# A causal convolution in a loop of 12 outputs from four half-size convolutions, with loads apart from transposes and four weight sums by ScalarE and accumulating DMA

## The chip, the core and the metric

The kernel runs on one core of a Trainium2 chip. A core has a matmul engine (TensorE, PE in the profile; its weight loads are PEld), three engines for elementwise work (VectorE is DVE, ScalarE is ACT, GpSimd is POOL), an engine that issues transfers (SyncE, SP) and 16 DMA engines. They run side by side and wait for one another through semaphores. The on-chip memory SBUF has 128 partitions. Matmul results land in PSUM, which has eight banks of 512 fp32 numbers per partition. The metric is device time in microseconds (us). "Span" is the time from the first to the last instruction of one profiled execution.

## What is computed

```python
# x [8, 4096, 512] f32, kernel [8, 512, 512] f32
def reference(x, kernel):
    out = np.zeros_like(x)
    for k in range(8):
        shifted = x delayed by k positions, zeros in front
        out += np.matmul(shifted, kernel[k])
    return out
```

This is a causal convolution over 4096 positions with 8 taps, in which each tap is a 512 x 512 matrix. Both kernels cut the 8 x 4096 positions into 128 runs of 256, one run per partition. One step of time, for all 128 runs at once, is a 128 x 512 matrix. Multiplied by one weight matrix it is called a *product* here: 4 matmuls of 128 x 128 by 128 x 512, one for each quarter of the inner 512.

## The kernel before

Eight outputs with eight taps would take 64 products. The kernel saves some of them by sums. A *node* is a convolution of 4 outputs with 4 taps, half the size, and it takes 9 products instead of 16 (names `a1 a0 u v0 v1 l00 l01 l10 l11`). Three nodes make 8 outputs: LO and HI, which work on sums of inputs with the lower and upper taps, and MID, which works on the inputs with the taps' difference. Four of the outputs are LO plus MID, the other four HI minus MID. In exchange, VectorE makes the sums of inputs and of results. All is bf16 but the results.

```python
def product(bank, comp, w, start):                 # 4 matmuls into one PSUM bank (line 197)
    for c in range(DC):
        nc.tensor.matmul(bank, lhsT=comp[:, c * P:(c + 1) * P], rhs=w[:, c, :],
                         start=start and c == 0, stop=c == DC - 1, skip_group_check=True)

def tt(o, a, b, op):                               # each VectorE sum (line 76)
    nc.vector.tensor_tensor(out=o, in0=a, in1=b, op=op)

def load_x(i, h):                                  # 4 steps of x, fp32 to bf16, into SBUF; 2 buffers
    xin[i, h] = xpool.tile([P, 4, D], bf, name="xin")
    load(xin[i, h], xr[:, K * i + 4 * h:K * i + 4 * h + 4, :])     # gpsimd DMA (line 80)

def transpose_x(i, h):                             # SBUF to SBUF, by DMA
    nc.sync.dma_start_transpose(
        out=XT[:, 4 * h:4 * h + 4, :].rearrange("p j (c m) -> p (j c) m", m=P),
        in_=xin[i, h].rearrange("p j d -> p (j d)"))

def node_seed(n, b_):                              # ScalarE: PSUM to PSUM, 512 wide
    n.p[b_] = pair((2 * n.k + b_) % 3)             # two banks; three pairs go round, a fourth is q
    ...
def node_d(n, b_):                                 # VectorE: difference in PSUM, 512 wide
    ...
def node_e(n, b_):                                 # results out of PSUM
    ...
    elif n.a == MID:
        ms[b_] = mpool.tile([P, 2, D], f32, name="ms")
        nc.scalar.copy(out=ms[b_], in_=p)
    else:
        tt(y, p, ms[b_], ADD if n.a == LO else SUB)                # 1024 wide, fp32
        store(n.i, n.a, b_, y)

# --- cut: the start, in which the first 16 outputs (6 nodes) are laid out by hand ---
for k, (i, a) in enumerate(order):                 # one turn is one node's slot
    ...
    node_l(cur, 0, LO); node_l(cur, 0, HI)         # products of this node ...
    node_a0(nxt); node_u(nxt)                      # ... mixed with those of the next
    node_l(cur, 1, LO); node_e(cur, 0)
    node_seed(nxt, 0); node_seed(nxt, 1); node_dts(nxt)
    ...                                            # prep_*: 39 rows of 512 bf16 summed per 8 outputs
    node_v(nxt, b_); node_d(nxt, b_)               # for b_ in 0, 1
    node_l(cur, 1, HI); node_a1(k + 2); node_e(cur, 1)
```

Of the kernel before, what the change touches and what calls it, by code (L numbers as in the profile page):

```python
# [8 lines left out]

LO, HI, MID = 0, 1, 2


@with_exitstack
def kernel(
# [13 lines left out]
    NIT = RUN // K  # L37
    assert K == 8 and D == 512 and S % RUN == 0 and RUN % K == 0
# [13 lines left out]
    xpool = ctx.enter_context(tc.tile_pool(name="x", bufs=2))  # L52

    ctx.enter_context(tc.manual_schedule())

    W = {}
    for a in (LO, HI, MID):
        for b_ in (LO, HI, MID):
            for c_ in (LO, HI, MID):
                W[a, b_, c_] = wpool.tile([P, DC, D], bf, name=f"w{a}{b_}{c_}")  # L60

    XT = spool.tile([P, K, D], bf, name="XT")
    D4 = spool.tile([P, K, D], bf, name="D4")
    D42 = spool.tile([P, K, D], bf, name="D42")
    D421 = spool.tile([P, K, D], bf, name="D421")
    D41 = spool.tile([P, 4, D], bf, name="D41")
    D2 = spool.tile([P, 5, D], bf, name="D2")
    D21 = spool.tile([P, 4, D], bf, name="D21")
    D1 = spool.tile([P, 2, D], bf, name="D1")

    F21 = spool.tile([P, 4, D], bf, name="F21")
    F0 = spool.tile([P, D], bf, name="F0")
    A1 = spool.tile([P, 2, D], bf, name="A1")
# [4 lines left out]

    def load(out, src):
        nc.gpsimd.dma_start(out=out, in_=src)  # L80

    xin = {}

    def load_x(i, h):
        xin[i, h] = xpool.tile([P, 4, D], bf, name="xin")
        load(xin[i, h], xr[:, K * i + 4 * h:K * i + 4 * h + 4, :])

    def transpose_x(i, h):
        nc.sync.dma_start_transpose(
            out=XT[:, 4 * h:4 * h + 4, :].rearrange("p j (c m) -> p (j c) m", m=P),  # L90
            in_=xin[i, h].rearrange("p j d -> p (j d)"))


    def pairs(z):
        return z.rearrange("p (a b) d -> p a (b d)", b=2)

    def prep_m():

        tt(D1[:, 0:2], XT[:, 7::-7], XT[:, 0:2], ADD)
        tt(pairs(D2[:, 1:5]), pairs(XT)[:, 3::-3], pairs(XT)[:, 0:2], ADD)  # L100

    def prep_d27():
        tt(D2[:, 0], XT[:, 5], XT[:, 7], ADD)

    def prep_d21():
        tt(D21[:, 0:4], D2[:, 0:4], D2[:, 1:5], ADD)

    def prep_d4(h):
        a, b = (XT[:, 4:8], XT[:, 0:4]) if h == LO else (XT[:, 0:4], XT[:, 4:8])
        tt(D4[:, 4 * h:4 * h + 4], a, b, ADD)  # L110

    def prep_d41(h):
        if h == LO:
            tt(D41[:, 0:2], D4[:, 7::-7], D4[:, 0:2], ADD)
        else:
            tt(D41[:, 2:4], D4[:, 3:5], D4[:, 4:6], ADD)

    def prep_d42(h):
        if h == LO:
            tt(pairs(D42)[:, 0:2], pairs(D4)[:, 3::-3], pairs(D4)[:, 0:2], ADD)  # L120
        else:
            tt(D42[:, 4:8], D4[:, 2:6], D4[:, 4:8], ADD)

    def prep_d421(h):
        if h == LO:
            tt(D421[:, 0:4:2], D42[:, 7:0:-6], D42[:, 0:4:2], ADD)
            tt(D421[:, 1:4:2], D42[:, 0:4:2], D42[:, 1:4:2], ADD)
        else:
            tt(D421[:, 4:8], D42[:, 3:7], D42[:, 4:8], ADD)

    ppool = ctx.enter_context(tc.tile_pool(name="p", bufs=1, space=PSUM))

    def pair(k):
        return ppool.tile([P, 2, D], f32, name=f"pp{k}")

    H, HF = XT, D421.bitcast(f32).rearrange("p (t b) d -> p t (b d)", b=2)
    nc.sync.dma_start(out=HF, in_=xr[:, RUN - 4:RUN, :])
    load_x(0, 0)
    zero = spool.tile([P, D], bf, name="zero")
    nc.vector.memset(zero, 0.0)  # L145
    U1 = zero
# [5 lines left out]
    def mid(level, u, v):  # L152

        if level == 0:
            return W[MID, u, v], W[HI, u, v], W[LO, u, v]
        if level == 1:
            return W[u, MID, v], W[u, HI, v], W[u, LO, v]
        return W[u, v, MID], W[u, v, LO], W[u, v, HI]

    def mid_dve(*which):  # L160
        o, u, v = mid(*which)
        tt(o, u, v, SUB)


    def mid_neg(u, v):
        nc.scalar.mul(out=W[MID, u, v], in_=W[LO, u, v], mul=-1.0)

    def mid_acc(u, v):
        nc.gpsimd.dma_start(out=W[MID, u, v], in_=W[HI, u, v], accum_op=ADD)

    load_w(4)
    load(H[:, 1:4], xr[:, RUN - 7:RUN - 4, :])
    ident = spool.tile([P, P], bf, name="ident")
    make_identity(nc, ident)
    bank = {}

    def fill(pw):

        for h in range(2):
            nc.tensor.matmul(pw[:, h], lhsT=zero[:, 0:P], rhs=zero, start=True, stop=True)  # L180

# [7 lines left out]

    for k in range(6):  # L190
        fill(pair(k % 4))
    XF = D42


    def product(bank, comp, w, start):
        for c in range(DC):
            nc.tensor.matmul(bank, lhsT=comp[:, c * P:(c + 1) * P], rhs=w[:, c, :],  # L197
                             start=start and c == 0, stop=c == DC - 1,
                             skip_group_check=True)

    mpool = ctx.enter_context(tc.tile_pool(name="m", bufs=2))
    cpool = ctx.enter_context(tc.tile_pool(name="c", bufs=2))
    fpool = ctx.enter_context(tc.tile_pool(name="f", bufs=2))
    ypool = ctx.enter_context(tc.tile_pool(name="y", bufs=4))

    class Node:
        pass

    def streams(i, a):

        if a == MID and i == 0:
            return (F0, [D1[:, 0], D1[:, 1]], [D2[:, 1], D2[:, 3]],
                    [F21[:, j] for j in range(4)])
        if (i, a) == (1, MID):
            return (U1, [A1[:, 0], A1[:, 1]], [D21[:, 0], D21[:, 2]],
                    [F21[:, j] for j in range(4)])
        if a == MID:
            return (XT[:, 0], [D1[:, 0], D1[:, 1]], [D2[:, 1], D2[:, 3]],
                    [D21[:, j] for j in range(4)])
        o = 4 * a  # L220
        if (i, a) == (1, LO):
            return (T4[:, 0], [D41[:, 0], D41[:, 1]], [T42[:, 0], T42[:, 2]],
                    [D421[:, j] for j in range(4)])
        if (i, a) == (1, HI):
            return (D4[:, 4], [D41[:, 2], D41[:, 3]], [D42[:, 4], D42[:, 6]],
                    [D421[:, j] for j in range(4)])
        return (D4[:, o], [D41[:, 2 * a], D41[:, 2 * a + 1]], [D42[:, o], D42[:, o + 2]],
                [D421[:, o + j] for j in range(4)])

    def node_a1(k):
        n = Node()
        nodes.append(n)
        n.k, (n.i, n.a) = k, order[k]
        a = n.a  # L240
        n.s = streams(n.i, a)
        n.q = pair(3)
        product(n.q[:, 1], n.s[1][1], W[a, MID, HI], True)
        nc.scalar.copy(out=n.q[:, 0], in_=n.q[:, 1])  # L244
        n.p = {}

    def node_a0(n):
        product(n.q[:, 0], n.s[1][0], W[n.a, MID, LO], False)

    def node_u(n):  # L250
        product(n.q[:, 1], n.s[0], W[n.a, MID, MID], False)

    def node_seed(n, b_):
        n.p[b_] = pair((2 * n.k + b_) % 3)
        if b_ == LO:
            nc.scalar.copy(out=n.p[b_][:, 1], in_=n.q[:, 1])  # L256
        else:
            nc.scalar.mul(out=n.p[b_][:, 1], in_=n.q[:, 1], mul=-1.0)  # L258

    def node_dts(n):  # L260
        n.dts = cpool.tile([P, D], f32, name="dts")
        nc.scalar.copy(out=n.dts, in_=n.q[:, 0])  # L262

    def node_v(n, b_):
        product(n.p[b_][:, 1], n.s[2][b_], W[n.a, b_, MID], False)

    def node_d(n, b_):
        p = n.p[b_]
        if b_ == LO:
            tt(p[:, 0], n.dts, p[:, 1], SUB)  # L270
        else:
            nc.vector.scalar_tensor_tensor(out=p[:, 0], in0=p[:, 1], scalar=-1.0,  # L272
                                           in1=n.dts, op0=MUL, op1=SUB)

    ms = {}

    def node_l(n, b_, j):
        product(n.p[b_][:, j], n.s[3][2 * b_ + j], W[n.a, b_, j], False)

    def store(i, a, b_, y):  # L280
        t0 = K * i + 4 * a + 2 * b_
        nc.sync.dma_start(out=orr[:, t0:t0 + 2, :], in_=y)

    first = {}

    def node_y(n, b_, a):
        y = first[n.i, a, b_]
        tt(y, y, n.p[b_], ADD if a == LO else SUB)

    def node_e(n, b_):  # L290
        p = n.p[b_]
        if n.k < 4:
            pool, name = ((mpool, "ms"), (ypool, "y"), (fpool, "f"), (ypool, "y"))[n.k]
            y = pool.tile([P, 2, D], f32, name=name)
            nc.scalar.copy(out=y, in_=p)  # L295
# [40 lines left out]
    def first_run(z):  # L336

        nc.vector.memset(z[:, :, 0:D:G], 0.0)  # L338

# [308 lines left out]
```

## Time and profile before

| | |
|---|---|
| median of 3 runs | 779.75 us (779.15 to 779.77) |
| span of the profiled run | 777.3 us |
| TensorE busy | 766.8 us, 99% |
| VectorE busy | 657.5 us, 85% |
| ScalarE busy | 284.9 us, 37% |
| transposes (SyncE's queue) | 61, median 6.1 us from issue to landing |
| loads of x (GpSimd's queue) | 64 of 512 KB, median 5.9 us |

A line of groups reads: source line, engine, operation, output tile <- input tiles, partitions x elements and type, count, then busy time in us and mean ns of one, then the engine's idle time just before such instructions and what ended it. A line of the timeline reads: start in us, duration in us, engine, line, operation. A line of the chain in order of time reads: start, length, and what was running. A queue's line has its packets, its MB and its packets' time as a share of the 16 DMA engines' span.

### The profile page before, as it was taken

Reading aid. Unit: us, or ns where it says so; the run is one execution under the profiler, and the core shown is the slowest. Engines: PE = TensorE matmul, PEld = TensorE weight load, DVE = VectorE, ACT = ScalarE, POOL = GpSimd, SP = SyncE. Lnnn points to the kernel's source line nnn. Section 1 sums busy time; section 2 is a strip of 40 time slices with the busy share of each in tenths; the row PEclk is TensorE's granted clock in tenths of the full one; section 3 lists DMA queues with packets and bytes.
Section 4 is the critical chain, followed back from the end, with each engine's and each line's share of the span. In section 5 each row is a group of like instructions: output and inputs, shape, how many; then the busy total and the mean of one; then the engine's idle time right before and its main releaser. Section 6 shows DMA issues by size and latency. Waiting matters only on the chain.

```text
span 777.3 us, 9450 instructions
## 1 busy us (share of the span) xinstructions
PE 766.8 (99%) x3584; PEld 347.3 (45%) x3584; DVE 657.5 (85%) x766; ACT 284.9 (37%) x462; POOL 42.3 (5%) x80
## 2 busy tenths in 40 slices
PE   7999999999999999999999999999999999999997
PEld 3444444444444444444444444444444444444443
DVE  4999988898888898888898888898888898888895
ACT  3553343333343333343333343333343333343332
POOL 4000000000000000000000000000000000000000
PEclk9999999999999999999999999999999999999999
DMA  9986878868786877787877878877697867687843
GB/s 199 211 125 170 226 185 178 208 159 190 164 199 163 197 172 189 164 198 169 194 171 187 164 174 190 207 162 188 163 187 176 207 158 190 165 186 179 204 133 121
DMA packets 159373, 139.42 MB, mean 179 GB/s; under 512 B 130144, under 2 KB 134240, under 8 KB 159200
## 3 DMA queue, kind: packets, MB, share of 16 engines
q1 hardware_dynamic: 145456, 99.89, 46.1%
q0 software_dynamic: 13728, 38.67, 31.6%
q8 instruction: 28, 0.46, 0.2%
q10 hardware_dynamic: 144, 0.26, 0.1%
q14 instruction: 17, 0.14, 0.1%
HBM read 77.33 MB, written 67.11 MB: 186 GB/s over the span
## 4 chain that ended last, share of the span: by engine, by line
PE 96%; DMA 2%; POOL 1%; ACT 0%; issue 0%; DVE 0%; DVEq 0%; POOLq 0%
PE pp L197 96%; DMA xin<-in_x_dram 2%; POOL w L80 0%; PE pp L186 0%; ACT y L295 0%; DVE y L76 0%; DVE pp L76 0%; POOL xin L80 0%; DVEq L647 0%; ACT pp L256 0%; ACT pp L244 0%; POOL XT L80 0%; PE pp L180 0%; POOL ident masks.py:199 0%; POOL ident masks.py:197 0%
## 5 line engine op out<-in xcount | busy, mean ns | idle before, releaser
L197 PE MATMUL pp<-w,D 128*128 128x512 bf16 x3280 | 715.5, 379 | 1.3 <-DVE w L76 0.9
L197 PEld LDWEIGHTS <-D 128*128 128x128 bf16 x3280 | 320.4, 98 | 389.8 <-issue 2.8
L76 DVE TENSOR_TENSOR D<-D 128x1024 bf16<-128x1024 bf16 (+1 forms) x252 | 228.2, 945 | 1.6 <-ACT D L353 1.6
L76 DVE TENSOR_TENSOR y<-pp,ms 128x1024 f32<-128x1024 f32 (+1 forms) x121 | 146.5, 1212 | 45.5 <-PE pp L197 45.4
L76 DVE TENSOR_TENSOR D<-XT 128x2048 bf16<-128x2048 bf16 (+2 forms) x153 | 142.1, 946 | 8.5 <-DMA XT<-xin 6.7
L244 ACT COPY pp<-pp 128x512 f32<-128x512 f32 x95 | 54.1, 570 | 256.0 <-PE pp L197 256.0
L256 ACT COPY pp<-pp 128x512 f32<-128x512 f32 x95 | 54.1, 570 | 170.6 <-PE pp L197 167.6
L76 DVE TENSOR_TENSOR pp<-dts,pp 128x512 f32<-128x512 f32 x95 | 65.5, 690 | 46.2 <-ACT dts L262 44.6
L299 ACT COPY ms<-pp 128x1024 f32<-128x1024 f32 x60 | 61.0, 1016 | 33.1 <-PE pp L197 33.1
L80 POOL DMA_DIRECT2D xin<-in_x_dram x64 | 34.2, 535 | 688.3 <-DMA XT<-xin 670.6
L272 DVE SCALAR_TENSOR_TENSOR pp<-pp,dts 128x512 f32<-128x512 f32 x95 | 65.9, 693 | 3.2
L262 ACT COPY dts<-pp 128x512 f32<-128x512 f32 x95 | 57.4, 604 | 2.0 <-PE pp L197 2.0
L258 ACT ACTIVATE pp<-pp 128x512 f32<-128x512 f32 x95 | 56.0, 589 | 1.2 <-DVE y L76 1.2
L197 PE MATMUL pp<-w,XT 128*128 128x512 bf16 x120 | 30.8, 379 | 0.0
L76 DVE TENSOR_TENSOR w<-w,w 128x2048 bf16<-128x2048 bf16 x18 | 21.6, 1219 | 0.4 <-DMA w<-in_kernel_dram 0.2
L197 PEld LDWEIGHTS <-XT 128*128 128x128 bf16 x120 | 11.7, 98 | 14.2
L180 PE MATMUL pp<-zero 128*128 128x512 bf16 x24 | 8.9, 505 | 2.4 <-DVE zero L145 1.2
L197 PE MATMUL pp<-w,w 128*128 128x512 bf16 x36 | 9.0, 379 | 1.3 <-ACT pp L244 0.7
L197 PE MATMUL pp<-w,F 128*128 128x512 bf16 x36 | 8.9, 379 | 0.0
L338 DVE MEMSET D<- 128x64 bf16 x2 | 0.2, 112 | 8.2 <-ACT D L351 7.7
L80 POOL DMA_DIRECT2D w<-in_kernel_dram x8 | 6.0, 766 | 0.8 <-DMA w<-in_kernel_dram 0.8
L197 PEld LDWEIGHTS <-w 128*128 128x128 bf16 x36 | 3.5, 97 | 5.8 <-issue 2.1
(55 smaller groups left out, 70.6 us busy)
## 6 DMA issues: line engine op xcount, KB each, us to landing
out_dram<-y SPq DMA_DIRECT2D x123, 512.0 KB, 3.5
xin<-in_x_dram POOLq DMA_DIRECT2D x64, 512.0 KB, 5.9
w<-in_kernel_dram POOLq DMA_DIRECT2D x8, 512.0 KB, 15.9
D<-in_x_dram SPq DMA_DIRECT2D x1, 1024.0 KB, 4.9
out_dram<-ms SPq DMA_DIRECT2D x2, 512.0 KB, 4.2
out_dram<-f SPq DMA_DIRECT2D x2, 512.0 KB, 3.7
XT<-xin SPq DMA_TRANSPOSE x61, 6.1
w<-w POOLq DMA_DIRECT2D x1, 512.0 KB, 9.9
```

Source lines behind the costliest of these rows:

```text
L76: nc.vector.tensor_tensor(out=o, in0=a, in1=b, op=op)
L80: nc.gpsimd.dma_start(out=out, in_=src)
L180: nc.tensor.matmul(pw[:, h], lhsT=zero[:, 0:P], rhs=zero, start=True, stop=True)
L197: nc.tensor.matmul(bank, lhsT=comp[:, c * P:(c + 1) * P], rhs=w[:, c, :], start=start and c == 0, stop=c == DC - 1, skip_group_check=True)
L244: nc.scalar.copy(out=n.q[:, 0], in_=n.q[:, 1])
L256: nc.scalar.copy(out=n.p[b_][:, 1], in_=n.q[:, 1])
L258: nc.scalar.mul(out=n.p[b_][:, 1], in_=n.q[:, 1], mul=-1.0)
L262: nc.scalar.copy(out=n.dts, in_=n.q[:, 0])
L272: nc.vector.scalar_tensor_tensor(out=p[:, 0], in0=p[:, 1], scalar=-1.0, in1=n.dts, op0=MUL, op1=SUB)
L299: nc.scalar.copy(out=ms[b_], in_=p)
L338: nc.vector.memset(z[:, :, 0:D:G], 0.0)
```

## The change

The loop now makes 12 outputs per turn from four nodes of 4 outputs x 4 taps: PL (with the sum of the two halves of the taps), MI (with their difference), H1 and H0 (with one half each). The 12 outputs follow from the four results with factors of one half. The first three nodes have 9 products as before. H0 is a *leaf*: it skips the last level of sums and the `d` step and has 11 products. The first 16 outputs are still made by hand-laid nodes, and three of those six are leaves now. This is meant to lower the number of products per output.

Loads of x go to tiles of their own in device memory (`xd`), and the transposes read from there into a ring `XR` of 20 steps. A load thus no longer waits for the transpose that empties its buffer, and SBUF is free for the nine more weight matrices of PL. Four of these (the sums of two tap matrices) are a ScalarE copy followed by an adding DMA; the other sums of weights are VectorE's. The diff below is shortened, and its comments are added.

```diff
-    NIT = RUN // K
+    HEAD, STEP, R = 2 * K, 12, 20
+    NB = (RUN - HEAD) // STEP
...
-    xpool = ctx.enter_context(tc.tile_pool(name="x", bufs=2))
+    ypool = ctx.enter_context(tc.tile_pool(name="y", bufs=5))
+    dpool = ctx.enter_context(tc.tile_pool(name="xd", bufs=NB * STEP // 4, space=bass.MemoryType.DRAM))
...
+    def load_x(t):
+        if t < RUN:
+            xd[t] = dpool.tile([P, 4, D], bf, name="xd")
+            rows(xd[t], t, 4)
+    def behind(z):                     # holds GpSimd's loads back until z is written
+        nc.gpsimd.tensor_copy(out=junk, in_=z[:, 0:2])
...
+    def node_z(n):                     # VectorE, from the ring; two pieces where it wraps
+        t = n.t
+        if n.a == PL:   zsum(0, t - 3, t + 1, 7, ADD)
+        elif n.a == MI: zsum(4, t + 1, t - 3, 7, SUB)
+        elif n.a == H1: zsum(0, t - 7, t + 1, 7, SUB)
+        else:           zsum(7, t, t + 8, 4, SUB)
+    def node_A(n):
+        tt(AX[n.k % 2], n.z[:, n.o + 2:n.o + 4], n.z[:, n.o + 3:n.o + 5], ADD)
+    def node_s(n):
+        tt(SX[n.k % 2], n.z[:, n.o:n.o + 5], n.z[:, n.o + 2:n.o + 7], ADD)
+    def node_F(n, b_):                 # not in a leaf
+        ...
+            tt(F[:, 2 * b_:2 * b_ + 2], s[:, 2 * b_:2 * b_ + 2], s[:, 2 * b_ + 1:2 * b_ + 3], ADD)
...
     def node_l(n, b_, j):
+        if n.leaf:
+            for c_ in (LO, HI):
+                product(o, comps(n)[2][2 * b_ + j + c_], W[n.a, b_, c_], False)
+        else:
+            product(o, comps(n)[3][2 * b_ + j], W[n.a, b_, j], False)
...
     def node_e(n, b_):                 # 12 outputs from the four results
+        elif n.a == PL:
+            nc.scalar.mul(out=cc[b_], in_=p, mul=0.5)
+        elif n.a == MI:
+            nc.vector.scalar_tensor_tensor(out=dd[b_], in0=p, scalar=-0.5, in1=cc[b_], op0=MUL, op1=ADD)
+        elif n.a == H1:
+            tt(y, p, dd[b_], ADD)      # stored
+        else:
+            tt(dd[b_], dd[b_], p, SUB) # stored
+    def middle(n, b_):
+        nc.vector.scalar_tensor_tensor(out=cc[b_], in0=cc[b_], scalar=2.0, in1=dd[b_], op0=MUL, op1=SUB)  # stored
...
+    def seed_plus(b_, c_):
+        nc.scalar.copy(out=W[PL, b_, c_], in_=W[H1, b_, c_])
+    def add_h0(a, b_, c_):
+        nc.gpsimd.dma_start(out=W[a, b_, c_], in_=W[H0, b_, c_], accum_op=ADD)
...
+    SLOT = {   # what each node's slot issues, in order; z, A, a1 are for the node after the next
+        PL: "s l00 F1 a0 l01 u l11 e0 s0 s1 dt F0 z x A v0 d0 v1 d1 l10 a1 e1",
+        MI: "l00 s F1 a0 l01 u l11 e0 s0 s1 dt F0 z x A v0 d0 v1 d1 l10 a1 e1",
+        H1: "l00 s F1 a0 l01 u l11 e0 s0 s1 dt F0 z A r g0 v0 d0 v1 d1 l10 e1",
+        H0: "l00 s F1 b1 l01 a0 u l11 e0 s0 s1 dt F0 z x A g1 v0 d0 v1 d1 l10 a1 e1",
+    }
+    # x: two transposes in PL's slot, one in MI's; r: behind(...) and three loads, two blocks ahead; g0, g1: middle
```

The start is cut here. Its loads now come in this order: x steps 0 to 3 and 4 to 7, the last steps of the runs (for the runs that follow), taps 4 and 5, x steps 8 to 11, taps 6, 7, 3, 1, 0, 2, x steps 12 to 15. Before, it was x steps 0 to 3, tap 4, the last steps, taps 6, 5, 7, x steps 4 to 7 and 8 to 11, taps 2, 0, 3, 1.

## The prediction, made before the changed kernel ran

> **What bounds the kernel now.** I read the page from the top: busy shares first, then the chain of work that ended last, then that chain in order of time.
>
> ```profile
> PE 766.8 (99%) x3584; PEld 347.3 (45%) x3584; DVE 657.5 (85%) x766; ACT 284.9 (37%) x462; POOL 42.3 (5%) x80
> PE 96%; DMA 2%; POOL 1%; ACT 0%; issue 0%; DVE 0%; DVEq 0%; POOLq 0%
> 5.96 18.30 DMA xin<-in_x_dram
> 45.87 726.95 PE pp L197 x3364
> ```
>
> TensorE (PE) carries 96% of the chain. From 45.87 us on, the chain is one unbroken stream of 3364 matmuls in 726.95 us, 0.2161 us each. Before that the start waits for its first loads. So the time is a count of matmuls times 0.2161 us, plus a start and a tail. Line 197 has 3280+120+36+36+8+4 = 3484 matmuls in its groups (the last two are small groups of the grouping by form); 120 of them lie before 45.87 us and are worth 25.9 us. The start therefore costs 45.87 - 25.9 = 20.0 us without products, the tail 777.3 - 772.8 = 4.5 us, and 20.0 + 3484 x 0.2161 + 4.5 = 777.4, the span. The median time lies 2.4 us above the span (779.75 against 777.3).
>
> VectorE (DVE) is second at 85%. Whether it can take over is the main question, so I read its groups by form and then its starts in order of time:
>
> ```profile
> L76 DVE TENSOR_TENSOR D<-D 128x2048 bf16<-128x2048 bf16 x123 | 147.3, 1217 | 0.0
> L76 DVE TENSOR_TENSOR y<-pp,ms 128x1024 f32<-128x1024 f32 x119 | 145.2, 1221 | 45.0 <-PE pp L197 44.9
> L76 DVE TENSOR_TENSOR D<-D 128x1024 bf16<-128x1024 bf16 x127 | 81.8, 682 | 1.6 <-ACT D L353 1.6
> L76 DVE TENSOR_TENSOR pp<-dts,pp 128x512 f32<-128x512 f32 x95 | 65.5, 690 | 46.2 <-ACT dts L262 44.6 <-PE pp L197 1.4
> ```
> ```profile
> 299.50 1.22 DVE L76 TENSOR_TENSOR D<-XT 128x2048 bf16<-128x2048 bf16 x1
> 300.63 1.22 DVE L76 TENSOR_TENSOR D<-D 128x2048 bf16<-128x2048 bf16 x1
> 301.77 0.69 DVE L76 TENSOR_TENSOR pp<-dts,pp 128x512 f32<-128x512 f32 x1
> 302.37 0.69 DVE L272 SCALAR_TENSOR_TENSOR pp<-pp,dts 128x512 f32<-128x512 f32 x1
> 302.97 1.21 DVE L76 TENSOR_TENSOR D<-XT 128x2048 bf16<-128x2048 bf16 x1
> ...
> 326.29 1.21 DVE L76 TENSOR_TENSOR D<-XT 128x2048 bf16<-128x2048 bf16 x1
> ```
>
> First column start, second duration. Starts lie closer than durations: an op of 1.22 us is followed 1.14 us later, one of 0.69 us 0.60 us later. So an op costs its duration less 0.08 us in a full queue. Where an op reads what the op right before it wrote, the step is the duration plus 0.04 (the copy at 25.41 us lasts 1.23, the sum that reads it starts at 26.67). 302.97 to 326.29 is one turn of the loop: 23.32 us for 108 matmuls, 0.2159 each.
>
> **What the Trainium skill says.** "VectorE: DVE Perf Modes", section "The perf-mode tier table", gives a two-input op two elements per cycle in bf16 (1224 ns for 2048) and one with any PSUM operand or fp32; the trace agrees (1217 ns; 1221 ns for 1024 fp32). Its section "The DRAIN you can't avoid" says each op pays a flush, so count matters, and that an op which is not held starts earlier; the trace has that as the 0.08 us. "TensorE: Matmul & The Clock Gate", section "Step-by-step: what each phase is for", has 216 ns between back-to-back 512-column matmuls: here 215.9. "DMA: Bandwidth & Descriptors", section "Why small descriptors are slow (HBM only)", warns of small packets to or from device memory; the transposes move packets of about 250 B (130144 packets under 512 B for 61 transposes of 512 KB, so some 2100 each), but from SBUF here, so no run yet shows whether it bites.
>
> **The change, part by part.** *Matmuls.* A product is 4 matmuls, 0.863 us. Before, 8 outputs take 3 nodes of 9 products. After, 12 outputs take three nodes of 9 (PL, MI, H1) and one leaf of 11 (H0): 38 products. The loop has 20 x 38 x 4 = 3040 matmuls. The head of 16 outputs has the direct node (64), three leaves (3 x 44) and two nodes (2 x 36): 268. Together 3308, 176 fewer, and 176 x 0.2161 = 38.0 us are saved if PE stays full. A block of 12 then takes 152 x 0.2159 = 32.8 us.
>
> *VectorE per block*, in start-to-start cost (bf16: 0.60 for 1024; 1.14 for 2048; 0.87, 1.41 and 1.95 for 1536, 2560 and 3584 on the same slope of 0.27 us per 512; fp32: 0.60 for 512, 1.14 for 1024): six F sums 3.6; four S sums 5.6; four A sums 2.4; six d ops 3.6; the z sums 7.05 (over 20 blocks 44 of 2048, 36 of 3584, 24 of 1536, as the ring wraps); eight fp32 output ops 9.1. That is 31.4, and four A sums that read the z just written add 4 x 0.12. So 31.9 us against 32.8: VectorE goes from 85% to about 97% and just stays under PE. Per output the sums grew (65 rows per 12 against 39 per 8), the d ops fell, and a middle result needs an extra fp32 op.
>
> *Slot by slot* the two do not balance. PE has 7.8, 7.8, 5.2 and 12.1 us in the slots of PL, MI, H1 and H0; VectorE 6.5, 7.9, 8.1 and 9.3. It falls behind by about 3 us over MI and H1 and catches up in H0. Laid out by hand, with H1's slot starting at 0 and VectorE 0.8 late: it evicts H1's first pair to 3.95, ScalarE then seeds the leaf by 5.2 (leaf wanted at 6.9: fine), A of the next PL is ready at 6.65 against 6.9 when PE wants it, all later ones have over half a microsecond, and VectorE is 0.8 late again one block on. So PE-bound is possible, with a slack of 0.25 us at the tightest place. That is less than hand-over between engines can cost, so I charge 0.25 us per block: 5 us.
>
> *ScalarE per block*: 3 nodes of four 512 copies (2.3 us each), two 1024 seeds and a 512 op in the leaf (2.6), two scaled 1024 copies (2.0): 11.6 of 32.8. It does not bind.
>
> *Transposes.* Before:
>
> ```profile
> q1 hardware_dynamic: 145456, 99.89, 46.1%
> q0 software_dynamic: 13728, 38.67, 31.6%
> xin<-in_x_dram POOLq DMA_DIRECT2D x64, 512.0 KB, 5.9
> XT<-xin SPq DMA_TRANSPOSE x61, 6.1
> ```
>
> Loads and transposes share the queues' 78% and each load waits for the transpose that frees its tile. After, a load goes to its own tile in device memory, two blocks early, so that wait is gone; but it was no engine's bound. The transpose gets a new source, read a second time. Two transposes are issued after H1's z (PL's slot) and needed by the next PL's z in H1's slot, about 14 us later. Two in a row at SPq's 4.2 us issue and 6.1 us landing take some 10 to 11. They fit unless the new source is a third slower.
>
> *Start.* Four weight sums leave VectorE for a ScalarE copy (1.9 us) and a DMA (9.9 us to landing in this trace). Behind the first x, two MB-size x loads and the 3/4 MB tail rows now stand ahead of the first weight. In the trace some 7.75 MB had landed by 24.3 us, about 0.36 MB per us after 2 us of latency. The first weight (4.75 MB in) then lands near 15 us, not 11.4; the fourth (8.75 MB) near 26. By then 7 products are done (6.0 us), which leaves 20.2 us lost against 16.6 at the same point before, whose later waits made it 20.0. I take 22 us, plus 2 us for the first PL weights arriving late.
>
> *Sum.* 22 + 3308 x 0.2161 (714.9) + 4.5 + 2 + 5 = 748.4 of span, plus 2.4: **751 us**, 3.7% faster.
>
> **The rivals.** *PE stays the only bound*: no block waits and the start costs what it did: 20.0 + 714.9 + 4.5 + 2.4 = 742. For it: the slots were ordered with sums split and spread, and the hand layout closes. *VectorE becomes the bound*: it loses 3.4 us of 23.3 waiting now (45.0 + 46.2 us over the kernel), and may afford under 1 in 32.8. If waits cost 1.2 us per block beyond my charge, 24 us more: 775, level with before. Against it: those waits are those of an engine with time to spare. *The transpose from device memory is slow*: at 9 us landing, z waits some 3 us per block, and VectorE cannot make it up: +60 us, 810. Against it: the queues are 78% busy and the window is two slots. *The start eats part of it*: +5 to 8 us.
>
> **Range and chances.** 742 is a floor. Half a microsecond more per block, or a start 8 us worse, gives about 760; both together 767. Range 742 to 766. Over 2% faster means below 764.2: 0.85. Within 2% takes the VectorE rival in earnest: 0.11. Slower by 2% takes the slow transpose: 0.04.
>
> **What would show it.** Right: the chain still over 93% PE, DVE near 93 to 95% busy by page, 32.8 to 33.3 us between like instructions 12 outputs apart, landing of transposes near 6 us. Wrong: DVE or DMA with several per cent of the chain; PE idle before line 118 for DVE; z waiting for DMA; blocks over 34 us; the first product later than 18 us. Fewer than 38 us saved with full blocks would put the loss in the start.

## The result, and the profile after

| | before | after |
|---|---|---|
| median of 4 runs | 779.45 us (778.88 to 779.77) | 757.88 us (757.45 to 759.61) |
| span of the profiled run | 777.3 us | 757.9 us |
| matmuls of products | 3484 | 3308 |
| 12 outputs in the loop | 34.98 us (1.5 x 23.32) | 32.90 us |
| share of the chain held by TensorE | 96% | 88% |

The ratio is 0.9729, 95% interval 0.9716 to 0.9743: 2.7% faster. 751 us had been predicted, with a range of 742 to 766. The page of the changed kernel: busy time by engine, three rows of the forty slices, and the chain that ended last.

```profile
PE 733.4 (97%) x3352; PEld 330.7 (44%) x3420; DVE 692.0 (91%) x727; ACT 255.0 (34%) x380; POOL 62.1 (8%) x103
PE   6999689999999999999999999999999999999997
DVE  1774899999999999999999999999999999999996
PEclk9999899999999999999999999999999999999999
PE 88%; DVE 5%; DMA 4%; issue 1%; ACT 1%; POOL 0%; DVEq 0%; ACTq 0%; POOLq 0%
```

From slice 7 to the last but one both rows read 9: TensorE and VectorE are both full, as foretold. The losses stand in slices 1, 5 and 6, that is up to 20 us and from some 76 to 114 us, and in slice 5 the clock dips too. (Of 3420 matmuls issued, of which 76 are transposes and 36 fillers on zeros at the start, the trace recorded 3352. Where I count matmuls below, I take the program's count.)

Operations and transfers of the same page; the last three lines are issues with their median us to landing:

```profile
L82 DVE TENSOR_TENSOR Z<-XR 128x3584 bf16<-128x3584 bf16 (+2 forms) x104 | 147.2, 1434 | 4.1 <-DMA XR<-xd 4.1
L82 DVE TENSOR_TENSOR S<-Z 128x2560 bf16<-128x2560 bf16 x80 | 118.6, 1483 | 0.0
L247 DVE SCALAR_TENSOR_TENSOR y<-pp,y 128x1024 f32<-128x1024 f32 x40 | 48.8, 1220 | 18.2 <-PE pp L118 17.2
out_dram<-y SPq DMA_DIRECT2D x124, 512.0 KB, 7.8
xd<-in_x_dram POOLq DMA_DIRECT2D x60, 512.0 KB, 10.7
XR<-xd SPq DMA_TRANSPOSE x60, 5.1
```

Transposes from device memory land in 5.1 us, faster than the 6.1 us from SBUF before. The loads and the stores pay instead: loads went from 5.9 to 10.7 us, stores from 3.5 to 7.8 us. In the loop VectorE waits for a store once, 2.0 us at 748 us, and for no load. The sum S of 2560 elements lasts 1483 ns, a step of 1.40, where 1.41 was taken. VectorE's one regular wait is the first output op of MI's slot, 17.2 us over 20 blocks. A piece of VectorE's timeline in the steady loop (start, duration, and in brackets the idle time before the op and what ended it):

```profile
402.72 0.69 DVE L82 TENSOR_TENSOR pp<-DT,pp 128x512 f32<-128x512 f32 x1
403.32 0.69 DVE L207 SCALAR_TENSOR_TENSOR pp<-pp,DT 128x512 f32<-128x512 f32 x1
403.92 1.48 DVE L82 TENSOR_TENSOR S<-Z 128x2560 bf16<-128x2560 bf16 x1
405.32 0.68 DVE L82 TENSOR_TENSOR F<-S 128x1024 bf16<-128x1024 bf16 x1
407.02 1.23 DVE L247 SCALAR_TENSOR_TENSOR y<-pp,y 128x1024 f32<-128x1024 f32 x1 [1.02 <-PE pp L118]
...
433.02 2.02 DVE L82 TENSOR_TENSOR Z<-XR 128x3584 bf16<-128x3584 bf16 x1
435.14 0.69 DVE L82 TENSOR_TENSOR A<-Z 128x1024 bf16<-128x1024 bf16 x1
435.75 0.69 DVE L82 TENSOR_TENSOR pp<-DT,pp 128x512 f32<-128x512 f32 x1
```

The op at 402.72 comes again at 435.75. An A that reads the z just written starts 0.10 us after that z's end (435.14 against 433.02 + 2.02), where 0.04 was taken. Averaged over 15 blocks by GpSimd's small copy, which runs once in each (155.74 to 649.30), a block is 32.90 us. TensorE's 152 matmuls at 0.2159 are 32.82. So a block loses 0.08 us, and VectorE is idle about 1 us in it.

What is left is the *head*, the first 16 outputs with the start of the first block. Busy time of each engine in four stretches of 10 us; after the stretch and its length stand PE, PEld, DVE, ACT and POOL with counts, then the granted clock, the DMA engines' share and GB/s:

```profile
60.00:70.00 10.00, 9.90 (x46) 4.52 (x47) 7.14 (x9) 4.09 (x6) 0.00 (x0) 1.00 1.03 178
70.00:80.00 10.00, 7.43 (x34) 3.30 (x34) 5.87 (x7) 3.79 (x4) 0.00 (x0) 1.00 0.37 63
80.00:90.00 10.00, 7.55 (x23) 2.79 (x23) 9.42 (x11) 3.44 (x4) 1.83 (x4) 0.66 0.98 249
90.00:100.00 10.00, 6.44 (x28) 2.60 (x27) 8.49 (x9) 2.23 (x4) 2.25 (x4) 1.00 1.04 235
```

40 us at 0.2161 would hold 185 matmuls; 131 are recorded. The chain in order of time (start, length, what) shows what held it:

```profile
66.29 9.02 DMA XR<-xd
...
75.40 1.24 DVE Z L82
...
81.01 1.14 DVE w L82
...
82.17 9.31 DMA out_dram<-w
...
91.51 1.23 DVE w L82
```

A transpose takes 9 us, VectorE works 7 us, a store takes 9 us, and VectorE goes on. Until 122.8 us no matmul is in the chain, although TensorE is full again from 100 us on (busy for 9.83 us from 100 to 110 us, 9.95 from 110 to 120). The timeline has the same as a row of waits:

```profile
75.40 1.23 DVE L82 TENSOR_TENSOR Z<-XR 128x2048 bf16<-128x2048 bf16 x1 [4.10 <-DMA XR<-xd]
...
81.11 0.58 ACT L190 ACTIVATE pp<-pp 128x512 f32<-128x512 f32 x1 [3.20 <-DVE y L82]
...
81.74 3.57 PE L118 MATMUL pp<-w,S 128*128 128x512 bf16 x8 [3.89 <-ACT pp L190]
...
91.51 1.23 DVE L82 TENSOR_TENSOR w<-w,w 128x2048 bf16<-128x2048 bf16 x1 [2.09 <-DMA out_dram<-w]
...
99.69 1.02 PE L118 MATMUL pp<-w,F 128*128 128x512 bf16 x3 [1.64 <-DVE pp L82]
```

The z of a node waits 4.1 us for rows of the ring. VectorE works in order, so an output sum behind that z is late, ScalarE's seed behind it, and TensorE stands 3.89 us. The 8 matmuls after that stand take 3.57 us, where 8 take 1.89 elsewhere, and the next 4 take 1.91 instead of 1.03: half speed. Then a weight sum waits 2.1 us, because its target still holds a result that is being stored.

### The profile page after: what moved, and what is told of

The parts are those of the page before. It is cut to its first block, busy times and chain, and to the rows that moved or that the text cites. A ratio compares the mean times of both kernels' runs of the same rounds, so it can differ in the third digit from the quotient of the medians.

```text
span 757.9 us, 8920 instructions
## 1 busy us (share of the span) xinstructions
PE 733.4 (97%) x3352; PEld 330.7 (44%) x3420; DVE 692.0 (91%) x727; ACT 255.0 (34%) x380; POOL 62.1 (8%) x103
## 4 chain that ended last, share of the span: by engine, by line
PE 88%; DVE 5%; DMA 4%; issue 1%; ACT 1%; POOL 0%; DVEq 0%; ACTq 0%; POOLq 0%
PE pp L118 87%; DMA w<-in_kernel_dram 2%; DMA out_dram<-w 1%; DMA XR<-xd 1%; DVE y L82 1%; DVE Z L82 1%; DVE S L82 1%; DVE w L82 1%; PE pp L295 0%; DVE F L82 0%; DVE pp L207 0%; PE pp L300 0%; DVE y L247 0%; DVE pp L82 0%; ACT pp L188 0%
## 5 line engine op out<-in xcount | busy, mean ns | idle before, releaser
L118 PE MATMUL pp<-w,S 128*128 128x512 bf16 x1114 | 261.6, 381 | 5.7 <-ACT pp L190 3.9
L118 PE MATMUL pp<-w,F 128*128 128x512 bf16 x973 | 248.4, 379 | 2.9 <-DVE pp L82 1.6
L118 PE MATMUL pp<-w,A 128*128 128x512 bf16 x668 | 173.1, 380 | 3.3 <-ACT pp L169 0.7
L118 PEld LDWEIGHTS <-S 128*128 128x128 bf16 x1136 | 111.1, 98 | 140.9 <-issue 9.5
L82 DVE TENSOR_TENSOR Z<-XR 128x3584 bf16<-128x3584 bf16 (+2 forms) x104 | 147.2, 1434 | 4.1 <-DMA XR<-xd 4.1
L118 PEld LDWEIGHTS <-F 128*128 128x128 bf16 x992 | 96.8, 98 | 119.4 <-issue 1.9
L82 DVE TENSOR_TENSOR S<-Z 128x2560 bf16<-128x2560 bf16 x80 | 118.6, 1483 | 0.0
L172 ACT COPY pp<-pp 128x512 f32<-128x512 f32 x62 | 35.3, 570 | 201.6 <-PE pp L118 201.6
L118 PE MATMUL pp<-w,Z 128*128 128x512 bf16 x378 | 96.8, 379 | 1.1 <-DVE w L82 0.6
L82 DVE TENSOR_TENSOR F<-S 128x1024 bf16<-128x1024 bf16 x124 | 83.2, 684 | 0.0
L247 DVE SCALAR_TENSOR_TENSOR y<-pp,y 128x1024 f32<-128x1024 f32 x40 | 48.8, 1220 | 18.2 <-PE pp L118 17.2
## 6 DMA issues: line engine op xcount, KB each, us to landing
xd<-in_x_dram POOLq DMA_DIRECT2D x60, 512.0 KB, 10.7
```

The costliest lines, as they stand in the source:

```text
L247: nc.vector.scalar_tensor_tensor(out=dd[b_], in0=p, scalar=-0.5, in1=cc[b_], op0=MUL, op1=ADD)
```

## The experiments

The theory after the result: *TensorE bounds the loop as predicted, and the loss is made in the head by transfers that land late in full queues.* Rivals: VectorE already bounds the loop; it is VectorE's own work that makes the head long; and the four sums by adding DMA, or the late first weights, cost the head its time. For loads apart from transposes the question was whether they bring anything. Each kernel is the changed one with the edit shown.

| run | median us (range) | ratio to before, 95% |
|---|---|---|
| changed kernel | 757.88 (757.45 to 759.61) | 0.9729 (0.9716 to 0.9743) |
| no_middle | 757.78 (757.23 to 759.7) | 0.9724 (0.9707 to 0.9742) |
| A_twice | 808.92 (806.69 to 810.5) | 1.037 (1.0344 to 1.0395) |
| no_leaf | 804.13 (802.86 to 805.0) | 1.0309 (1.0292 to 1.0326) |
| sbuf_rows | 762.05 (760.78 to 765.07) | 0.9776 (0.9753 to 0.98) |
| w4_first | 757.35 (756.43 to 758.53) | 0.9712 (0.9699 to 0.9725) |
| x20_early | 755.4 (755.11 to 757.71) | 0.9693 (0.9679 to 0.9707) |
| loads_sorted | 755.4 (754.36 to 759.92) | 0.9697 (0.9675 to 0.9719) |
| plus_by_dve | 757.88 (757.03 to 758.85) | 0.9722 (0.9707 to 0.9737) |
| plus_early | 757.13 (756.16 to 757.73) | 0.9714 (0.9701 to 0.9728) |
| quiet_head | 761.79 (760.38 to 763.08) | 0.9774 (0.9761 to 0.9788) |
| quiet_plus | 761.28 (759.71 to 763.28) | 0.977 (0.9754 to 0.9785) |
| quiet_held | 758.28 (756.87 to 759.78) | 0.973 (0.9717 to 0.9744) |

Runs of one of these kernels differ by 1.6 to 5.6 us, those of the kernel before by 0.9 to 1.7. A difference of 1 us between two rows says nothing.

### The loop: less and more work for VectorE

**no_middle** leaves out the two middle ops of each block: 2.3 us of VectorE's work less, and the middle four outputs of each block go out without them.

```diff
     def middle(n, b_):
-        nc.vector.scalar_tensor_tensor(out=cc[b_], in0=cc[b_], scalar=2.0,
-                                       in1=dd[b_], op0=MUL, op1=SUB)
         store(n.t + 4 + 2 * b_, cc[b_])
```

> Leaves out the VectorE op that makes the middle four outputs of each block (2 ops, 2.28 us start to start per block; those outputs hold half of PL's result instead). Theory (TensorE bounds the loop, VectorE has just room): the block shortens by no more than the 0.08 us that it loses now, so 756 to 758 us. Rival (VectorE bounds the loop): up to 2 us per block, 720 us or less.

Measured: 757.78 us, and a block of 32.91 us (153.21 to 646.82 over 15). Taking VectorE work away changes nothing, so VectorE does not bound the loop.

**A_twice** makes each A sum of the loop a second time: four ops of 0.60 us more per block.

```diff
-            "A": (two, lambda: node_A(two)),
+            "A": (two, lambda: (node_A(two), node_A(two))),
```

> Each A sum of the loop is made twice (four more ops of 0.60 us, 2.4 us per block). By the count, VectorE then needs 31.9 + 2.4 = 34.3 us, or some 0.1 more where the second waits for the first, against 32.8 of TensorE: VectorE becomes the bound, blocks of 34.3 to 34.8 us, 786 to 796 us. If the count of VectorE were too high and it had 2 us of room or more: 758 to 762 us.

Measured: 808.92 us, and a block of 35.46 us (160.41 to 692.32 over 15): 2.56 us more, which is above the range expected. The added work is more than 2.4 us, because the second A waits for the first, which writes the same tile. In the timeline of A_twice:

```profile
425.64 1.42 DVE L82 TENSOR_TENSOR A<-Z 128x1024 bf16<-128x1024 bf16 x2
426.97 0.69 DVE L82 TENSOR_TENSOR pp<-DT,pp 128x512 f32<-128x512 f32 x1
```

The pair takes 1.33 us from start to start, where one A takes 0.61 (435.14 to 435.75 in the changed kernel). So a second A costs 0.72 us, and four of them 2.9 us. The waits from 200 to 700 us, first of the changed kernel, then of A_twice (engine and line, what it waited for, us in total, times, longest):

```profile
DVE y L247 <- PE pp L118: 14.2, 15, 1.0
...
PEld L118 <- DVE A L82: 4.5, 15, 0.3
```
```profile
PEld L118 <- DVE A L82: 33.5, 30, 1.5
...
PE pp L118 <- DVE A L82: 19.4, 28, 1.0
PEld L118 <- DVE F L82: 17.0, 28, 0.6
...
DVE y L247 <- PE pp L118: 7.5, 14, 0.5
```

TensorE now waits for A and F several times a block, and VectorE still waits for TensorE half a microsecond in each. I had taken VectorE's idle microsecond for room that could be filled first (2.4 less 1.0). Only about half of it is: this wait falls from 0.95 to 0.54 us per block, and 2.9 us less 0.4 are the 2.5 us by which the block grew. The 0.3 us for which TensorE's weight load waits for A in each block of the changed kernel shows that A had no room ahead of it at all.

**no_leaf** makes H0 a node of 9 products in the loop, with two of MI's matrices standing in for the two that a leaf does not need. It has 8 matmuls (1.7 us) fewer per block, and four VectorE ops (two F, two d; 2.4 us) more.

```diff
+    W[H0, LO, MID], W[H0, HI, MID] = W[MI, LO, MID], W[MI, HI, MID]
...
-            self.leaf = k in LEAF or k >= 6 and a == H0
+            self.leaf = k in LEAF
```

> H0 in the loop becomes a node of 9 products like the others, with two F sums and two d ops (for the two weights that it lacks it takes two others of the same size, so four outputs per block are not the reference's). TensorE 36 x 4 x 0.2159 = 31.1 us per block, VectorE 31.9 + 2.4 = 34.3. Theory (VectorE then bounds): blocks of 34.3 to 34.8, 786 to 796 us. Rival (TensorE bounds and VectorE gives way): 31.1 to 31.5 us per block, 722 to 731 us.

Measured: 804.13 us, and a block of 35.25 us (157.92 to 686.61 over 15). Fewer matmuls and a longer time. The chain of the page:

```profile
DVE 50%; PE 38%; issue 7%; DMA 4%; ACT 1%; DVEq 0%; another core or an unknown queue 0%; ACTq 0%; POOLq 0%
```

Two edits that add 2.9 and 2.4 us of VectorE's work at different places lengthen the block by 2.56 and 2.35 us, so it is the work more than its place. (In no_leaf a part is TensorE's clock: TensorE stops for about 2.1 us in each block, and in six of the 20 blocks matmuls then run at half speed. The block from 157.92 us, in which they do, takes 35.72 us, the one from 193.64, in which they don't, 34.99.) Less VectorE work gains nothing, more of it costs nearly in full: at 32.90 us the loop stands where the two bounds meet, and the leaf is what keeps it on TensorE's side.

### Loads apart from transposes

**sbuf_rows** puts the loads of x back into two SBUF tiles, each waiting for the transpose that empties its tile. To make room, two weight sums of MI are left out and other weights stand in. The load of step 20 comes early, as in x20_early below, which is therefore its partner. The diff is shortened.

```diff
-    dpool = ctx.enter_context(tc.tile_pool(name="xd", bufs=NB * STEP // 4, space=bass.MemoryType.DRAM))
+    dpool = ctx.enter_context(tc.tile_pool(name="xd", bufs=2))
...
+    W[MI, LO, MID], W[MI, HI, MID] = W[MI, LO, LO], W[MI, HI, LO]
...
-                transpose_x(two.t + 12)
-                transpose_x(two.t + 16)
+                for d in (12, 16):
+                    transpose_x(two.t + d)
+                    load_x(two.t + d + 8)
```

> Undoes the loads apart from transposes: x goes to two SBUF tiles of 4 steps as before, each load waits for the transpose that empties its tile, and steps 20 to 23 load early (compare with the run with that alone). Room comes from leaving out two weight sums of MI (two other weights stand in). Theory (the loads were no bound): within 3 us of the early-load run, transposes near 6 us instead of 5. Rival (without the early loads a transpose comes late for the z sums of 14 us later): z waits for transposes in most blocks, 10 us or more slower.

Measured: 762.05 us, 6.6 us above x20_early. One op of the middle result starts at 117.53 and, 16 blocks on, at 651.45: 33.37 us per block against 32.90 (122.68 to 649.08 in the changed kernel). The first of the 16 takes 35.09 us, the other 15 take 33.26. That is 9 us over 20 blocks; a head some 3 us shorter than that of x20_early, with two sums left out, gives part of it back. Its transfers, and two waits in 200 to 700 us, one of VectorE and one of SyncE's queue:

```profile
out_dram<-y SPq DMA_DIRECT2D x124, 512.0 KB, 3.2
xd<-in_x_dram POOLq DMA_DIRECT2D x60, 512.0 KB, 6.6
...
XR<-xd SPq DMA_TRANSPOSE x60, 4.9
```
```profile
DVE y L83 <- DMA out_dram<-y: 6.4, 7, 1.9
...
SPq L96 <- DMA xd<-in_x_dram: 96.0, 15, 8.8
```

The source of the transpose makes no difference (4.9 from SBUF, 5.1 from device memory). z does not wait here, which the rival had expected, yet the time is not that of the theory either. Some output ops wait for the store that frees their buffer, although each store lands in half the time. The last line says why. SyncE issues transposes and stores in one order. Once in each block it waits some 6 us for a load, because that load could start only when the transpose before had emptied the tile, and a store that stands behind this transpose goes out late. The output sum that ends at 317.51 us is an example: its store goes out at 319.19, because a transpose is being issued from 315.74 to 319.10, and the next such sum waits 1.06 us for it. In x20_early this store goes out 0.03 us after its sum in each block. So loads apart are worth a third of a microsecond per block and 2 us in the first, through the order of SyncE's queue and not through faster transfers.

### The head: loads, weights and waits

**w4_first** takes the second x load behind the first weight.

```diff
-    load_xin(0, 4)
     rows(H[:, 1:4], RUN - 7, 3)
...
     load_w(4)
+    load_xin(0, 4)
```

> The load of x steps 4 to 7 goes behind the first weight instead of ahead of it. The start is set by the volume that must land before the fourth weight: then the first product starts some 3 us earlier (12 to 13 us against 15.5), but the time stays within 1 us of 757.9. Rival (the first product sets the start): 754 to 755 us.

Measured: 757.35 us, within 1 us of the changed kernel. Which of these two loads goes first does not matter to the time. The first product did not come earlier, though: the weight landed at 13.32 us instead of 15.41, but TensorE was at the transposes and fillers ahead of it until 15.42. What an earlier first product would be worth is therefore not shown.

**x20_early** moves one load up, **loads_sorted** puts all loads of the head in the order in which they are needed.

```diff
     load_x(16)
+    load_x(20)
     node_l(n1, 0, LO)
...
     node_e(n3, 0)
-    load_x(20)
     node_a0(n4)
```

> The load of x steps 20 to 23 moves up, directly behind that of steps 16 to 19; nothing else changes. Theory (the head gives time back because the first sum of the loop waits for a late load and its transpose, and VectorE, in order, drags ScalarE and TensorE with it): the wait of 4.1 us of a z sum for the transpose goes, with the 3.9 us stall of TensorE behind it and the slow-clock matmuls after that; 750 to 753 us against 757.9. Rival (the head is short of VectorE time or of weight sums anyway, and the wait only shows first): another wait takes its place, 756 to 758 us.

> As the run with the early load, and the loads of steps 24 to 51 stand in the order in which they are needed, where before steps 36, 44, 48 and 40 came ahead of 24, 28, 32. Theory of late loads: the transpose of steps 24 to 27, which took 7.6 us of issue at 99.5 us, comes clean as well, another 0 to 2 us; 749 to 752 us. Rival (bandwidth: the loads together are too much beside stores and adding transfers in this stretch, whatever their order): no gain over the early load alone, within 1 us of it.

Measured: 755.4 us both, 2.5 us better than the changed kernel and not the gain that a vanished wait would bring. In the timeline of x20_early:

```profile
65.00 4.75 SPq L95 DMA_TRANSPOSE XR<-xd  x1
...
73.43 1.23 DVE L82 TENSOR_TENSOR Z<-XR 128x2048 bf16<-128x2048 bf16 x1 [3.41 <-DMA XR<-xd]
```

z still waits 3.4 us. (The profiled run is the slowest of the four, 757.71 us. The others took 755.1 to 755.6 us at a mean clock of 0.996 to 1.000 instead of 0.992, so their stop of TensorE may have been shorter.) Though its load comes much earlier, the transpose is issued only 1.3 us earlier (66.29 before). It lands late because of its issue and of what lies beside it, not because of its load: the DMA engines' share in 60 to 70 us was 1.10 (1.03 in the changed kernel). SyncE's own waits show what holds the issue: it waits 13.4 us for TensorE. The rows that the transpose overwrites are read by a product that starts at 63.94 us here and at 65.23 in the changed kernel, and the transpose follows 1.06 us later in both, at that product's end.

**plus_by_dve** makes the four sums for PL by VectorE where the adding transfers were issued; **plus_early** places them where VectorE is idle for 6.6 us, before 59.7 us.

```diff
     def seed_plus(b_, c_):
-        nc.scalar.copy(out=W[PL, b_, c_], in_=W[H1, b_, c_])
+        pass
     def add_h0(a, b_, c_):
-        nc.gpsimd.dma_start(out=W[a, b_, c_], in_=W[H0, b_, c_], accum_op=ADD)
+        if a == PL:
+            tt(W[PL, b_, c_], W[H0, b_, c_], W[H1, b_, c_], ADD)
+        else:
+            nc.gpsimd.dma_start(out=W[a, b_, c_], in_=W[H0, b_, c_], accum_op=ADD)
```

> The four weight sums that ScalarE and adding transfers make go back to VectorE at the places of the transfers' issue; four more sums of 1.14 us in the head. Theory (VectorE in order is what the head runs on from 60 to 100 us): slower by 3 to 5 us, 761 to 763 us. Rival (the adding transfers crowd the queues and hold GpSimd's loads, 26 us of waits of GpSimd for ScalarE): the load of steps 20 to 23 comes earlier, and the time falls to 752 to 756 us.

The edit of plus_early (the calls of `seed_plus` and `add_h0` for PL go):

```diff
     wsum(MI, MID, MID)
+    plus((LO, HI), (HI, HI), (LO, LO), (HI, LO))
     node_a1(n4)
```

> The four PL weight sums are VectorE's again (no ScalarE copies, no adding transfers), and all four stand where VectorE waits for TensorE from 53 to 59.7 us; loads as in the changed kernel. Theory: they cost nothing there (4 x 1.14 = 4.6 us in 6.6 us of waiting), the transpose lands in time as in the run with these sums at the late places, where no z sum waited, and unlike there nothing is added later: 751 to 754 us. Rival (the stretch from 70 to 100 us is bound by something else): 756 to 758 us.

Measured: 757.88 and 757.13 us. Moving four sums to ScalarE and an adding DMA is worth nothing measurable. In both, z's wait is gone, with more room for the transpose in the queues (share in 60 to 70 us: 0.76 and 0.70). The time did not follow. The timeline of plus_early shows what came in its place:

```profile
88.81 1.23 DVE L82 TENSOR_TENSOR w<-w,w 128x2048 bf16<-128x2048 bf16 x1 [3.81 <-DMA out_dram<-w]
90.09 1.02 PE L118 MATMUL pp<-w,Z 128*128 128x512 bf16 x4 [3.15 <-DVE w L82]
```

VectorE arrives earlier at the weight sum, whose target is still being stored, and there it waits longer.

**quiet_head** holds the loads of later steps back, so that the queues are empty while the transpose runs. **quiet_plus** joins it with plus_early. **quiet_held** also moves the stored result to another place, so that this weight sum need not wait for the store. The first diff is shortened: the loads of steps 20 to 48 go from their old places.

```diff
     behind(AX[1][:, 0])
-    load_x(36)
+    load_x(24)
...
     behind(AX[0][:, 0])
+    load_x(28)
...
     node_F(n6, 0)
+    behind(F[:, 0])
+    for t in range(32, 52, 4):
+        load_x(t)
```

> Loads in the head alone: steps 20 to 23 early as before, steps 24 to 27 next, step 28 on only after the A sum of the loop's first node, and steps 32 to 51 held back until the first F sum of that node (by a tiny GpSimd copy that waits for it). The early load alone left the transpose of steps 20 to 23 at 65 us, since it overwrites rows that TensorE reads until then, and it took 8.4 us to land beside 5 MB of loads. Theory (crowded queues in the head, not the order of loads): it now lands in 5 us, no z sum waits, and the 3.2 us stall of TensorE behind it and the slow-clock matmuls go: 750 to 753 us. Rival (VectorE has too much to do between 70 and 100 us in any case): within 2 us of the early load's 755.4.

> Both: loads held back and the four sums in VectorE's waiting time. If crowded queues are the whole of it, no more than 1 us better than the better of the two; if the wait of a weight sum for a store (2.1 us near 90 us) is also the queues' doing, it goes as well: 748 to 751 us.

```diff
-    held = {(2, 1): WP[:, 8:12], (0, 0): WP[:, 12:16], (0, 1): WP[:, 16:20]}
+    held = {(2, 1): WP[:, 32:36], (0, 0): WP[:, 12:16], (0, 1): WP[:, 16:20]}
...
+    plus((LO, HI), (HI, HI), (LO, LO), (MID, MID))
...
+    plus((HI, LO))
```

> As the run with both, and the early result that lay in the place of PL's middle weight lies in the place of another one, which is needed later; so the middle weight's sum moves into the waiting time, and no sum waits for a store. The wait of 2.1 us of VectorE near 90 us and what TensorE loses behind it go: 2 to 3 us less than with both, 746 to 749 us. If that wait hid behind VectorE's other work: same as with both, within 1 us.

Measured: 761.79, 761.28 and 758.28 us. quiet_head and quiet_plus are 3 to 4 us slower than the changed kernel, quiet_held level with it; none brought the gain. Yet up to 93 us quiet_plus works: until then no z waits for a transpose, and the weight sum waits 0.3 us for its store. The timeline of quiet_plus:

```profile
90.58 2.55 POOL L88 DMA_DIRECT2D xd<-in_x_dram  x5
93.32 13.60 SPq L95 DMA_TRANSPOSE XR<-xd  x1
...
113.16 1.23 DVE L82 TENSOR_TENSOR Z<-XR 128x2048 bf16<-128x2048 bf16 x1 [6.64 <-DMA XR<-xd]
...
114.44 1.89 PE L118 MATMUL pp<-w,Z 128*128 128x512 bf16 x4 [5.78 <-DVE Z L82]
```

Its first product on F of the loop starts at 93.52 us, where the changed kernel has it at 99.69. Then the five loads that were held back go out together, a transpose beside them takes 13.6 us to issue, and the z after it waits 6.6 us, 2.5 more than the wait that was removed. quiet_head has the same wait at 6.1 us, quiet_held at 6.3. quiet_held is 3.0 us better than quiet_plus, the gain expected, but not for the reason given: the wait that it was to remove had shrunk to 0.3 us in quiet_plus already. In all three runs the five loads still land in the head, and where they do, a transpose is late.

quiet_held shows more. From 62 to 105 us none of the engines that compute waits for a transfer in it. Its engines from 70 to 100 us, and its first product on F of the loop:

```profile
70.00:80.00 10.00, 8.76 (x40) 3.79 (x39) 9.96 (x10) 3.61 (x6) 0.71 (x2) 1.00 0.53 103
80.00:90.00 10.00, 8.10 (x35) 3.31 (x35) 9.72 (x12) 2.24 (x5) 2.89 (x5) 1.00 0.70 266
90.00:100.00 10.00, 8.05 (x38) 3.40 (x36) 9.97 (x12) 2.52 (x4) 0.65 (x2) 1.00 0.97 196
...
92.29 1.02 PE L118 MATMUL pp<-w,F 128*128 128x512 bf16 x4 [1.83 <-DVE pp L82]
```

VectorE (the third pair) is full, and TensorE (the first) is not. From the product on the rows of the ring (63.75 us here, 65.23 in the changed kernel) to that product on F (92.29 and 99.69) lie 104 matmuls, worth 22.5 us. They take 34.5 us in the changed kernel and 28.5 here. So of the 12.0 us lost in this stretch, 6.0 stay when no transfer is late, and those are VectorE's own work in the order that it has there. Late transfers made the other half.

## Why the prediction was right, and which term was off

The sum again in its own terms, on the profiled run, which is the slowest of the four, with a span some 2 us above the others' (755.7 to 756.5). What is lost by a moment is the clock time less 0.2161 for each matmul of products done by then: 292 at 99.69 us, so 36.6 us.

| term | predicted | measured |
|---|---|---|
| start, with late PL weights | 22 + 2 = 24 | 36.6 |
| 3308 matmuls | 714.9 | 714.9 |
| hand-over, 20 blocks | 5 | 1.9 (the rest) |
| tail | 4.5 | 4.5 |
| span | 748.4 | 757.9 |
| median above the span | 2.4 | 1.7 |

The hand-over term was 3.1 us too high, which by luck covered a part of what the start had too little.

*Count of matmuls.* Right: 38 products in 12 outputs, and a loop held by TensorE. The chain over the whole span has 88% TensorE, not the 93% named as the test, with 5% VectorE and 4% DMA; these were named as signs of a wrong prediction, and they are the head's. VectorE's busy share is 91%, not 93 to 95. 176 matmuls fewer are worth 38.0 us; the head gave back 16.6 of them (36.6 against 20.0), the loop 1.9. That leaves 19.5, and the spans differ by 19.4.

*VectorE just under the bound.* Right, to a closer mark than could be claimed by hand. 31.9 us were counted per block; the trace has 32.90 less some 1.0 idle. no_middle and A_twice enclose it. The 0.25 us charged for hand-overs were 0.08, so VectorE as the bound, the rival with 775 us, did not come about; A_twice and no_leaf show that 2.4 to 2.9 us more work would have brought it, and more than it said.

*Transposes from device memory.* Right: near 6 us was said, 5.1 came, and sbuf_rows has nearly the same from SBUF (4.9). The section "Why small descriptors are slow (HBM only)" of "DMA: Bandwidth & Descriptors" in the Trainium skill was the reason for the rival of 810 us. For these packets of about 250 B its warning did not show in landing times. That the loads' wait for the transposes bounds no engine holds for the old loop; in the new one sbuf_rows shows it worth a third of a microsecond per block.

*Start.* First product at 15.54 us (near 15 was said), and 23.5 us lost by 46 us (22 was said): right so far, though by 26 us 4.5 products were done and not 7. The failing step is the next one, "plus 2 us for the first PL weights arriving late". After 46 us another 13 us are lost. It is the mis-sized term, and its name was wrong as well: PL's weights made by ScalarE and DMA were not the matter (plus_by_dve and plus_early change nothing). 5.5 of the 13 come up to 81.74 us, most of them TensorE's 3.89 us stand behind z and the seed. Another 3.4 come up to 87.73 us, 2.5 of them the 12 half-speed matmuls. The last 4.2, up to 99.69 us, are four shorter stops behind VectorE and ScalarE, the first of them for the late weight sum. By quiet_held about half of what is lost after 65 us is VectorE's own work, the other half late transfers. I had looked at the start as loads ahead of the first product and never laid out the head's 100 us, as I did for the loop. The rival that gave the start 5 to 8 us more was the one that came, larger. Two small sums are off as well and change nothing: 751 + 10 + 8 are 769, not 767, and 7.75 MB in 22.3 us are 0.35 MB per us.

*What stays open.* Whether VectorE's half of the loss in the head is a floor, or another order of its work would give it back; no run changed that order alone. Nor is any run free of late transfers through the whole head. The runs took the waits away one at a time, and each time a later one took its place: z's wait, then the weight sum's, then z of a later node. x20_early is the best version found, 755.4 us, and loads_sorted is level with it.

## What to carry to other kernels

When a change cuts the bound's own work, lay out the stretch ahead of the steady loop instruction by instruction as well: there this kernel gave back 16.6 of the 38.0 us that its fewer matmuls saved. Two full engines can meet so exactly that removing work from one gains nothing and adding it costs nearly all of it; test both directions before calling either the bound. A wait for a transfer that is taken away in a crowded stretch is worth little until one knows what waits next; holding loads back only moved the crowd here.

## What the runs showed of the hardware

- A stand of TensorE is paid twice. After 3.89 us without a matmul, 12 matmuls ran at half speed, the first 8 in 3.57 us in place of 1.89. quiet_plus, after 5.78 us, shows a granted clock of 0.66 for 110 to 120 us. After 1.6 us (99.69) the clock stayed at 1.00. The section "What's actually happening" of "TensorE: Matmul & The Clock Gate" in the Trainium skill says that the clock halves after an idle window of about 3.4 us. These three agree, but other runs show it after shorter stops. In plus_by_dve, after 2.05 us (82.99), 16 matmuls took 5.30 us in place of 3.62, and in plus_early, after 3.15 us (90.09), the clock was 0.83 for 90 to 100 us. In no_leaf a stop of 2.13 us (159.58) was followed by half speed (4 matmuls in 1.91 us at 161.95), one of 2.20 us (195.31) was not (4 in 1.03 at 196.16). The longest stop in quiet_held before 105 us, 1.83 us, left the clock at 1.00.
- A load into device memory in a group of three took 10.7 us to landing, in SBUF one at a time behind a transpose 6.6 us. Beside the former stores took 7.8 us, beside the latter 3.2.
- A transpose that lands in 5.1 us as a median was stretched to 9.0 us beside full queues, and its issue on SyncE to 13.6 us beside five loads.
